# The columns of v as a seven-product unit behind q, gate and k in one pass of eight accumulators, the recurrence beside r

## The chip, the cores and the metric

One NeuronCore of one Trainium2 chip. The metric is the device time of one execution of the program, in microseconds.

## What is computed

A block with two branches of 1024 columns on 512 tokens of width 2048, everything in float32. The parts that matter here, cut from the reference:

```python
h = rms_norm(x, norm_g)                       # (512, 2048)
proj = h @ w_in                               # h, b, c, z of the convolution, then q, k (512 each), v, r (1024 each), gate (16)
# gated linear attention, 4 heads, chunks of 64 tokens
glog = log_sigmoid(g_down @ w_up + b_gate) / 16
bcum = cumsum(glog, within a chunk);  b_end = bcum[:, :, -1]
k_dec = k * exp(b_end - bcum)
u = einsum('bnchk,bnchv->bnhkv', k_dec, v)    # one state update for each chunk
state = exp(b_end) * state + u                # a scan over the 8 chunks
o = einsum('bnchk,bnhkv->bnchv', q, state)    # then RMS norm for each head, times silu(r)
# convolution branch: silu(z) * b * conv3(c * h);  both are joined, times w_out, plus x, then a final RMS norm
```

## The kernel before

Every projection is done to float32 accuracy with products of a reduced type: each operand is split into a high part (a rounding on ScalarE) and a low part (a subtraction on VectorE, lines 116 and 117), and three matmuls (high x high, low x high, high x low) take the place of one. The transposed, gain-scaled input h stands in SBUF all the time as `hT_hi` and `hT_lo`, 16 k tiles of 128 rows by 512 tokens. RMS norm's factor for a token, `rstd`, is applied to results.

The work goes in stages, one behind the other on TensorE:

1. *The time-major stage* (`w_tm`, line 262): gate, k and v, 16 + 512 + 1024 = 1552 columns. Tokens are the output's rows, so h is the stationary operand. The columns are cut into four passes of 388. A pass walks the 16 k tiles, with four accumulators (one bank for each 128 tokens), and the four passes alternate between the two groups of four banks. The first pass also loads x transposed (`load_x`), the second loads x by tokens for the sums of squares (`token_stats`), behind which `token_rstd` gives rstd and `tm_out` scales the results.
2. *q and r* (`ft_unit`, lines 157 to 159): 4 + 8 blocks of 128 columns, with the weights stationary and 512 tokens moving. After each half of a block `step()` runs one step of the generator `gla_steps`: six steps of gates and decays, then for each pair of chunks the state products (`pair_state`, u), the splits of the next k and v, and the outputs (`pair_out`, o), then their transposes (tp). It starts its first state products after seven half blocks, in the fourth block of q. r's blocks go to DRAM (`r_raw`).
3. *Four seven-product units* (`st_unit`, line 592), for z with b and c with h. A unit treats a 512 x 2048 by 2048 x 1024 product as 2 x 2 blocks and makes it with seven block products in place of eight: pa, pb and pc with blocks of the weights as loaded (`raw_mm`), then, in four steps c, the products pd, pe, pa and pf on weight blocks that VectorE mixes by sums and differences (line 646). Sums of blocks of h are needed for them (`quarter_sums`, four sets, made at the end of r from a second load of x): the operands s1, s2 and s4 are split and kept, and s3 is put in the place of the second token half of h's first eight k tiles (`place_third`), which nobody needs any longer. A unit's results leave by `gate_cols` or `conv_cols`. Before its last products a unit calls `before_out`, which splits the first weights of what comes next.
4. *The output projection* (`w_out`): 512 columns, a fifth seven-product unit for 1024, 512 columns again, and the final norm.

All DMAs of weights and of x are issued by SyncE's queue in order. Tiles of 128 x 512 come from one pool of 44 slots (`k2`), weights from 8 raw slots of 128 x 1024 and 4 slots each for their high and low parts (`SPLITBUFS`). PSUM's eight banks form two groups, `acc` and `aux`, of four. The text's order gives priorities; the framework's scheduler lays out each engine's queue from them when the program is built, and each engine serves its queue in that order. A tile that has no free slot waits for one.

Of the kernel before, what the change touches and what calls it, by code (L numbers as in the profile page):

```python
# [30 lines left out]
CH = 8  # L31
KPC = KT // CH
TMW = RANK + DK + GW
TMB = 4
TMC = TMW // TMB
UNIT = KPC * S
# [3 lines left out]
GST = 80  # L40
WARM = 9
# [3 lines left out]
STC = 4  # L45
HT = S // 2
# [3 lines left out]
def hybrid_block(ctx: ExitStack, tc: tile.TileContext, xT, x, params, w_tm, w_ft, w_st, w_up, b_gate, w_out, final_g, out):  # L50
# [68 lines left out]
    def raw_tile(name):  # L119
        return wpool.tile([P, UNIT], F32, tag="raw", name=f"raw_{name}", bufs=RAWBUFS)  # L120
# [16 lines left out]
    def load_split_fine(src, name):  # L137
        raw, (hi, lo) = raw_tile(name), split_tiles(name)

        def piece(i):  # L140
            sl = slice(i * TMC, (i + 1) * TMC)
            nc.sync.dma_start(out=raw[:, sl], in_=src[:, sl])
            (nc.scalar.copy if i else nc.vector.tensor_copy)(out=hi[:, sl], in_=raw[:, sl])
            nc.vector.tensor_sub(out=lo[:, sl], in0=raw[:, sl], in1=hi[:, sl].bitcast(F32))

        return hi, lo, piece

# [73 lines left out]
    def tm_out(b, pst):  # L221
        for tt in range(TT):
            c0 = b * TMC
            while c0 < (b + 1) * TMC:
                if c0 < RANK:
                    c1, dst = RANK, gd[:, tt, :]
                else:
                    j = (c0 - RANK) // S
                    c1 = min(RANK + (j + 1) * S, (b + 1) * TMC)
                    o0 = c0 - RANK - j * S  # L230
                    dst = kv[tt][j][:, o0 : o0 + c1 - c0]
                nc.vector.tensor_scalar(
                    out=dst, in0=pst[tt][:, c0 - b * TMC : c1 - b * TMC],
                    scalar1=rstd[:, tt : tt + 1], scalar2=None, op0=ALU.mult,
                )
                c0 = c1

    for b in range(TMB):
        pst = [(acc if b % 2 else aux)(f"tm{b}_{tt}") for tt in range(TT)]
        for c in range(CH):  # L240
            if b == 0:
                hi, lo, piece = load_split_fine(w_tm[b, c], f"tm{b}_{c}")
                for i in range(KPC):
                    if c == 0 and i == 0:
                        with tc.high_priority():
                            load_x(0)
                    else:
                        load_x(c * KPC + i)
                    piece(i)
            else:  # L250
                hi, lo = load_split(w_tm[b, c], KPC * TMC, f"tm{b}_{c}")
            if b == 1:
                for k in (2 * c, 2 * c + 1):
                    token_stats(*divmod(k, HC))
            for i in range(KPC):
                kt = c * KPC + i
                xh, xl = h(kt)
                csl = slice(i * TMC, (i + 1) * TMC)
                wh, wl = hi[:, csl], lo[:, csl]
                for k, (a, w) in enumerate(((xh, wh), (xl, wh), (xh, wl))):  # L260
                    for tt in range(TT):
                        nc.tensor.matmul(  # L262
                            pst[tt][:, 0:TMC], lhsT=a[:, tt * P : (tt + 1) * P], rhs=w,
                            start=kt == 0 and k == 0, stop=kt == KT - 1 and k == 2,
                        )
        if b == 0:
            first = pst
            gate_weights()
            continue
        if b == 1:  # L270
            token_rstd()
            tm_out(0, first)
            gate_inputs()
        tm_out(b, pst)


    rps = aux("rps")
# [6 lines left out]
    nc.tensor.matmul(rps, lhsT=onesr, rhs=dh, start=True, stop=False)  # L284
    nc.tensor.matmul(rps, lhsT=onesr, rhs=dl, start=False, stop=True)
    nc.scalar.copy(out=rB, in_=rps)


    def ft_unit(u):
# [146 lines left out]
    def gla_steps():  # L436
        ga = gate_transpose()
        yield
        gl = []
        for tt in range(TT):  # L440
            gl.append(gate(tt, ga))
            if tt % 2:
                yield
        for tt in range(TT):
            gate_decay(tt, gl[tt])
            if tt % 2:
                yield
        chunk_decays()
        chunk_splits(0)
        yield  # L450
        done = None
        for tt in range(TT):
            pair_state(tt)
            yield
            if done is not None:
                out_transpose(tt - 1, done)
            if tt + 1 < TT:
                chunk_splits(tt + 1)
            yield
            done = pair_out(tt)  # L460
            yield
        yield
        out_transpose(TT - 1, done)
# [27 lines left out]
    def r_block(b):  # L491
        r = ft_unit(HEADS + b)
        t1 = t2(f"r1_{b}")
        nc.vector.tensor_mul(out=t1, in0=r, in1=rB)
        nc.scalar.activation(t1, t1, AF.Silu)
        nc.sync.dma_start(out=r_raw[b], in_=t1)

    for hh in range(HEADS):
        q = ft_unit(hh)
# [9 lines left out]
        qs.append(parts)  # L509

# [24 lines left out]
    def quarter_sums(j):  # L535
# [7 lines left out]
        made = sums(*raws, j, "qs")  # L543
        for k in (4, 1, 2):
            s_parts[k][j] = split_small(made[k], f"qp{k}_{j}")
        s_parts[3][j] = made[3]

# [5 lines left out]

    for b in range(8):
        r_block(b)
        if b >= 6:
            for j in range(2):
                quarter_sums(2 * (b - 6) + j)
    for _ in steps:
        pass  # L560
# [13 lines left out]
    def st_source(u, c, q):  # L574
        return w_st[u, c, q] if u < 4 else w_out[1 + q % 2, STC * (q // 2) + c]
# [24 lines left out]
    def st_unit(u, factor, out, before_out, into=None, between=()):  # L600
        main, side = (aux, acc) if u % 2 else (acc, aux)
# [22 lines left out]
        if u == 0:  # L624
            for j in range(STC):
                place_third(j)
# [15 lines left out]
        for c in range(STC):  # L642
# [94 lines left out]
    def early_tail(f):  # L737
# [7 lines left out]
        return go  # L745

# [228 lines left out]
def _layout(x, norm_g, w_in, conv_w, conv_b, gla_w_up, gla_b_gate, gla_norm_g, w_out, final_g):  # L975
# [7 lines left out]
    tm = np.concatenate([g, k, v], axis=2)  # L983
    tm = tm.reshape(CH, KPC, P, TMB, TMC).transpose(3, 0, 2, 1, 4).reshape(TMB, CH, P, KPC * TMC)
# [9 lines left out]
    st = np.stack([unit(a[:, :, s], b[:, :, s]) for s in halves for a, b in ((cz, cbb), (cc, ch))])  # L994
# [42 lines left out]
```

## Time and profile before

| what | value |
|---|---|
| device time, median of 3 runs | 786.15 us (786.07 to 786.17) |
| the profiled execution: its own time, its span | 785.95 us, 783.6 us |
| TensorE busy, matmuls | 773.7 us, 3752 matmuls |
| VectorE, ScalarE, GpSimdE busy | 563.7, 379.9, 31.6 us |
| DMA | 140.39 MB, 179 GB/s over the span |

The span runs from the first to the last instruction; the profiled execution's own time is 2.35 us longer. Matmuls overlap in their pipeline, so a row's duration is longer than the distance to the next matmul. PE is TensorE, PEld its weight loads, DVE VectorE, ACT ScalarE, POOL GpSimdE, SP SyncE. A tile's name stands without its number.

### The profile page before, as it was taken

Reading aid. Unit: us, or ns where it says so; the run is one execution under the profiler, and the core shown is the slowest. Engines: PE = TensorE matmul, PEld = TensorE weight load, DVE = VectorE, ACT = ScalarE, POOL = GpSimd, SP = SyncE. Lnnn points to the kernel's source line nnn. Section 1 sums busy time; section 2 is a strip of 40 time slices with the busy share of each in tenths; the row PEclk is TensorE's granted clock in tenths of the full one; section 3 lists DMA queues with packets and bytes.
Section 4 is the critical chain, followed back from the end, with each engine's and each line's share of the span. In section 5 each row is a group of like instructions: output and inputs, shape, how many; then the busy total and the mean of one; then the engine's idle time right before and its main releaser. Section 6 shows DMA issues by size and latency. Waiting matters only on the chain.

```text
span 783.6 us, 10104 instructions
## 1 busy us (share of the span) xinstructions
PE 773.7 (99%) x3752; PEld 664.8 (85%) x3752; DVE 563.7 (72%) x711; ACT 379.9 (48%) x574; POOL 31.6 (4%) x38
## 2 busy tenths in 40 slices
PE   9999999999999999999999999999999999999995
PEld 9999999887878888888888888888888888888885
DVE  7533242366666549998998699878987997997913
ACT  6552121373688757644543445345436345733504
POOL 1000000000000000000000000000000000004601
PEclk9999999999999999999999999999999999999998
DMA  8973343222232238778866556665666459578006
GB/s 309 324 272 84 105 130 120 96 84 80 80 107 82 95 108 285 261 224 284 312 204 192 197 184 207 188 213 174 204 189 184 124 180 368 190 196 295 20 1 215
DMA packets 48932, 140.39 MB, mean 179 GB/s; under 512 B 5826, under 2 KB 7874, under 8 KB 48884
## 3 DMA queue, kind: packets, MB, share of 16 engines
q1 hardware_dynamic: 48628, 139.74, 54.3%
q8 instruction: 29, 0.48, 0.3%
q14 instruction: 19, 0.16, 0.1%
q10 hardware_dynamic: 256, 0.02, 0.0%
HBM read 130.29 MB, written 9.44 MB: 178 GB/s over the span
## 4 chain that ended last, share of the span: by engine, by line
PE 96%; ACT 1%; DVE 1%; issue 1%; POOL 0%; ACTq 0%; POOLq 0%
PE tm L262 17%; PE pa L592 14%; PE pc L592 7%; PE pb L592 7%; PE pf L592 7%; PE pe L592 7%; PE pd L592 7%; PE ft L159 5%; PE ft L157 5%; PE ft L158 5%; PE po L159 3%; PE po L158 3%; PE po L157 3%; PE u L363 1%; PE warm L86 1%
## 5 line engine op out<-in xcount | busy, mean ns | idle before, releaser
L116 ACT CAST hi_sq_t<-raw_sq 128x1024 fp32r<-128x1024 f32 x80 | 84.3, 1055 | 119.7 <-PE pf L592 24.0
L117 DVE TENSOR_TENSOR lo_sq_t<-raw_sq,hi_sq_t 128x1024 fp32r<-128x1024 f32 x80 | 98.4, 1234 | 20.5 <-ACT hi_sq_t L116 20.4
L646 DVE TENSOR_TENSOR raw_sq<-raw_sq,raw_sq 128x1024 f32<-128x1024 f32 x80 | 97.2, 1220 | 7.6 <-DMA raw_sq<-in_w_st 6.4
L116 ACT CAST hi_st<-raw_st 128x1024 fp32r<-128x1024 f32 x60 | 63.2, 1054 | 67.7 <-PE pa L592 21.6
L117 DVE TENSOR_TENSOR lo_st<-raw_st,hi_st 128x1024 fp32r<-128x1024 f32 x60 | 72.1, 1220 | 13.7 <-ACT hi_st L116 13.5
L157 PE MATMUL ft<-hhi,hi_ft 128*128 128x512 f32 x192 | 75.7, 394 | 0.0
L159 PE MATMUL ft<-hhi,lo_ft 128*128 128x512 f32 x192 | 75.2, 392 | 0.0
L158 PE MATMUL ft<-hlo,hi_ft 128*128 128x512 f32 x192 | 75.1, 391 | 0.0
L117 DVE TENSOR_TENSOR lo_tm<-raw_tm,hi_tm 128x776 fp32r<-128x776 f32 x24 | 23.2, 966 | 58.7 <-ACT hi_tm L116 58.7
L262 PE MATMUL tm<-hi_tm,hhi 128*128 128x388 f32 x256 | 56.3, 342 | 0.1
L262 PE MATMUL tm<-hi_tm,hlo 128*128 128x388 f32 x256 | 55.6, 339 | 0.0
L262 PE MATMUL tm<-lo_tm,hhi 128*128 128x388 f32 x256 | 55.4, 338 | 0.0
L116 ACT CAST hi_tm<-raw_tm 128x776 fp32r<-128x776 f32 x24 | 20.2, 842 | 68.2 <-PE tm L262 64.7
L117 DVE TENSOR_TENSOR lo_ft<-raw_ft,hi_ft 128x1024 fp32r<-128x1024 f32 x24 | 29.4, 1223 | 27.3 <-ACT hi_ft L116 27.2
L262 PEld LDWEIGHTS tm<-hi_tm,hhi 128*128 128x128 f32 x256 | 46.4, 190 | 0.7 <-ACT hhi L169 0.4
L262 PEld LDWEIGHTS tm<-lo_tm,hhi 128*128 128x128 f32 x256 | 46.0, 188 | 0.0
L262 PEld LDWEIGHTS tm<-hi_tm,hlo 128*128 128x128 f32 x256 | 45.9, 188 | 0.0
L159 PEld LDWEIGHTS ft<-hhi,lo_ft 128*128 128x128 f32 x192 | 36.0, 188 | 7.8
L157 PEld LDWEIGHTS ft<-hhi,hi_ft 128*128 128x128 f32 x192 | 36.1, 188 | 7.6 <-issue 0.2
L158 PEld LDWEIGHTS ft<-hlo,hi_ft 128*128 128x128 f32 x192 | 36.1, 188 | 7.3
L851 POOL TENSOR_TENSOR res<-res,fg 128x512 f32<-128x512 f32 x12 | 21.8, 1850 | 449.0 <-DMA fg<-in_final_g 443.0
L157 PE MATMUL po<-hi_wo,yh 128*128 128x512 f32 (+1 forms) x104 | 39.6, 381 | 0.0
(279 smaller groups left out, 1649.7 us busy)
## 6 DMA issues: line engine op xcount, KB each, us to landing
raw_sq<-in_w_st SPq DMA_DIRECT2D x64, 512.0 KB, 4.3
raw_st<-in_w_st SPq DMA_DIRECT2D x48, 512.0 KB, 4.4
raw_ft<-in_w_ft SPq DMA_DIRECT2D x24, 512.0 KB, 3.4
raw_tm<-in_w_tm SPq DMA_DIRECT2D x24, 388.0 KB, 4.1
raw_sq<-in_w_out SPq DMA_DIRECT2D x16, 512.0 KB, 4.1
raw_wo<-in_w_out SPq DMA_DIRECT2D x13, 512.0 KB, 3.9
raw_st<-in_w_out SPq DMA_DIRECT2D x12, 512.0 KB, 7.8
rawx<-in_xT SPq DMA_DIRECT2D x16, 256.0 KB, 4.8
```

What stands on the lines that cost most here:

```text
L86: nc.tensor.matmul(wps[:, 0:P], lhsT=ones, rhs=ones, start=True, stop=True)
L116: nc.scalar.copy(out=hi, in_=full)
L117: nc.vector.tensor_sub(out=lo, in0=full, in1=hi.bitcast(F32))
L157: nc.tensor.matmul(ps, lhsT=ah, rhs=bh, start=first, stop=False)
L158: nc.tensor.matmul(ps, lhsT=ah, rhs=bl, start=False, stop=False)
L159: nc.tensor.matmul(ps, lhsT=al, rhs=bh, start=False, stop=last)
L262: nc.tensor.matmul(pst[tt][:, 0:TMC], lhsT=a[:, tt * P : (tt + 1) * P], rhs=w, start=kt == 0 and k == 0, stop=kt == KT - 1 and k == 2,)
L363: nc.tensor.matmul(us[j][:, vsl], lhsT=kp[a][rows, ksl], rhs=vp[b][rows, vsl], start=k == 0, stop=k == 2)
L592: nc.tensor.matmul(ps[t], lhsT=fs[t][part_], rhs=ww[:, sl], start=first and c == 0 and r == 0 and k == 0, stop=last and c == STC - 1 and r ...
L646: nc.vector.tensor_tensor(out=dst, in0=x0, in1=x1, op=op)
L851: nc.gpsimd.tensor_mul(out=res[tt][cbk], in0=res[tt][cbk], in1=fg[cbk])
```

## The change

The time-major stage keeps gate and k only, 528 columns. It is one pass: two accumulators of 264 columns for each 128 tokens, so all eight banks, and each k tile is used for both. Weights come in groups of three pieces of 264 columns (the first two groups piece by piece). x by tokens is loaded from the sixth k tile on (`STATS0`). The last two k tiles are done bank by bank, and each bank is emptied behind its own last matmul, half of them by ScalarE.

The q heads follow, with one set of quarter sums behind each. Then v goes through `st_unit` with the number `UV` = 5; `v_cols` scales its results by rstd. Inside it `place_third` overwrites half of h's first eight k tiles, as in unit 0, and `restore_quarter` loads that quarter of x again and writes h back, one set after each step's product with s3. r's first block begins with the upper k tiles. The recurrence's generator has two empty steps more, so that its first state products fall behind the first half of r's first block, and the splits of the first k and v stand in front of r. The row of rstd (`rms_row`) moves into its first step. The quarter sums for units 0 to 3 are made again at the end of r, as before.

```diff
-TMW = RANK + DK + GW
-TMB = 4
+TMW = RANK + DK
+TMB = 2
 TMC = TMW // TMB
+TMP = KT * TMB
+TMG = 3
...
+UV = 5
...
-    kv = [[t2(f"kv{tt}_{j}") for j in range(3)] for tt in range(TT)]
+    kv = [[t2(f"k{tt}"), None, None] for tt in range(TT)]
     gd = const.tile([P, TT, RANK], F32, name="gd")
...
+    tm_group = [None, None]
...
+    def tm_weights(p):
+        g, i = divmod(p, TMG)
+        sl = slice(i * TMC, (i + 1) * TMC)
+        if i == 0:
+            raw, (hi, lo) = raw_tile(f"tm{g}"), split_tiles(f"tm{g}")
+            tm_group[:] = hi, lo
+            c0, n = p * TMC, min(TMG, TMP - p) * TMC
+            if g > 1:
+                nc.sync.dma_start(out=raw[:, 0:n], in_=w_tm[:, c0 : c0 + n])
+                split(hi[:, 0:n], lo[:, 0:n], raw[:, 0:n])
             else:
...
+                for j in range(TMG):
+                    fine = slice(j * TMC, (j + 1) * TMC)
+                    nc.sync.dma_start(out=raw[:, fine], in_=w_tm[:, c0 + j * TMC : c0 + (j + 1) * TMC])
+                    (nc.scalar.copy if j else nc.vector.tensor_copy)(out=hi[:, fine], in_=raw[:, fine])
+                    nc.vector.tensor_sub(out=lo[:, fine], in0=raw[:, fine], in1=hi[:, fine].bitcast(F32))
...
+        if b == 0:
+            nc.vector.tensor_scalar(out=dst, in0=src, scalar1=rstd[:, tt : tt + 1], scalar2=None, op0=ALU.mult)
+        else:
+            nc.scalar.activation(dst, src, AF.Copy, scale=rstd[:, tt : tt + 1])
...
+    tm_banks = [[(aux if b else acc)(f"tm{b}_{tt}") for tt in range(TT)] for b in range(TMB)]
+
+    def tm_mm(kt, b, tt, w):
+        xh, xl = h(kt)
+        for k, (a, wi) in enumerate(((xh, w[0]), (xl, w[0]), (xh, w[1]))):
+            nc.tensor.matmul(
+                tm_banks[b][tt][:, 0:TMC], lhsT=a[:, tt * P : (tt + 1) * P], rhs=wi,
+                start=kt == 0 and k == 0, stop=kt == KT - 1 and k == 2,
+            )
+
+    tm_last = {}
+    for kt in range(KT):
+        if kt == 0:
+            with tc.high_priority():
+                load_x(0)
+        else:
+            load_x(kt)
+        if kt == 2:
             gate_weights()
...
+        if STATS0 <= kt < STATS0 + 8:
+            for k in (2 * (kt - STATS0), 2 * (kt - STATS0) + 1):
+                token_stats(*divmod(k, HC))
+        for b in range(TMB):
+            w = tm_weights(kt * TMB + b)
+            if kt >= KT - 2:
+                tm_last[kt, b] = w
+            else:
+                for tt in range(TT):
+                    tm_mm(kt, b, tt, w)
...
+    token_rstd()
...
+    for b in range(TMB):
+        for tt in range(TT):
+            for kt in range(KT - 2, KT):
+                tm_mm(kt, b, tt, tm_last[kt, b])
+            tm_out(b, tt)
+        if b == 0:
+            gate_inputs()
+
+
+    def rms_row():
...
+    def ft_unit(u, first=0):
         ps = acc(f"ft{u}")
-        for half in range(2):
-            n = KT // 2
-            hi, lo = load_split(w_ft[u, half], UNIT, f"ft{u}_{half}")
+        n = KT // 2
+        for half in (int(first), int(not first)):
+            hi, lo = ft_weights(u, half)
             for i in range(n):
                 kt = half * n + i
                 csl = slice(i * P, (i + 1) * P)
-                mm3(ps, (hi[:, csl], lo[:, csl]), h(kt), kt == 0, kt == KT - 1)
+                mm3(ps, (hi[:, csl], lo[:, csl]), h(kt), half == first and i == 0, half != first and i == n - 1)
...
     def gla_steps():
+        rms_row()
...
         chunk_decays()
-        chunk_splits(0)
+        yield
+        yield
...
+        r = ft_unit(HEADS + b, b == 0)
...
-    for hh in range(HEADS):
-        q = ft_unit(hh)
+    def q_head(hh):
+        q = ft_unit(hh, 0)
...
+    def quarter_sums(j):
+        made = sums(*quarter_raws(j), j, "qs")
...
+    def restore_quarter(j):
+        raw = t2(f"rq{j}").rearrange("p (i t) -> p i t", i=2)
+        nc.sync.dma_start(out=raw, in_=xT[:, 2 * j : 2 * j + 2, HT:S])
+        for i in range(2):
+            kt = 2 * j + i
+            c, r = divmod(kt, HPC)
+            nc.scalar.activation(hT_hi[c][:, r, HT:S], raw[:, i, :], AF.Copy, scale=g_in[:, kt : kt + 1])
+            nc.vector.scalar_tensor_tensor(
+                out=hT_lo[c][:, r, HT:S], in0=raw[:, i, :], scalar=g_in[:, kt : kt + 1],
+                in1=hT_hi[c][:, r, HT:S].bitcast(F32), op0=ALU.mult, op1=ALU.subtract,
+            )
...
-        main, side = (aux, acc) if u % 2 else (acc, aux)
+        main, side = (aux, acc) if u in (1, 3) else (acc, aux)
...
-        if u == 0:
+        if u in (0, UV):
...
+            if u == UV:
+                restore_quarter(c)
...
+    def v_cols(i, j, ts):
+        for t in range(2):
+            tt = 2 * i + t
+            nc.vector.tensor_scalar(out=ts[t], in0=ts[t], scalar1=rstd[:, tt : tt + 1], scalar2=None, op0=ALU.mult)
+            kv[tt][1 + j] = ts[t]
+
+    def next_rows():
+        for half in (1, 0):
+            ft_weights(HEADS, half)
+
+    for hh in range(HEADS):
+        q_head(hh)
+        quarter_sums(hh)
+    ahead_of(UV)()
+    st_unit(UV, h_factor, v_cols, next_rows)
+    chunk_splits(0)
+    for b in range(8):
+        r_block(b)
+        if b >= 6:
+            for j in range(2):
+                quarter_sums(2 * (b - 6) + j)
+    for _ in steps:
+        pass
```

## Rows read from the trace of the kernel before

**Rows 1.** The page: the span, and busy time, share and instructions of each engine.

```profile
span 783.6 us, 10104 instructions
PE 773.7 (99%) x3752; PEld 664.8 (85%) x3752; DVE 563.7 (72%) x711; ACT 379.9 (48%) x574; POOL 31.6 (4%) x38
```

**Rows 2.** TensorE's waits: what it waited for, us in total, times, longest.

```profile
PE warm L86 <- POOL ones L83: 1.1, 1, 1.1
PE o L391 <- ACT oT L432: 0.7, 1, 0.7
```

**Rows 3.** The chain that ended last, in order of time: start us, us, what.

```profile
5.40 136.58 PE tm L262 x768
...
230.72 1.54 PE u L363 x12
...
250.09 1.62 PE u L363 x24
...
299.22 10.88 PE pa L592 x48
...
331.86 2.72 PE pd L592 x12
...
375.38 6.35 PE pa L592 x28
```

**Rows 4.** Timeline of TensorE: the time-major stage's ends, then a run of 256 columns.

```profile
5.40 1.39 PE L262 MATMUL tm<-hi_tm,hhi 128*128 128x388 f32 x4
...
9.67 0.86 PE L262 MATMUL tm<-lo_tm,hhi 128*128 128x388 f32 x4
...
141.81 0.40 PE L284 MATMUL rps<-dg_hi,onesr 128*128 128x512 f32 x1
...
735.33 0.28 PE L157 MATMUL po<-hi_wo,yh 128*128 128x256 f32 x1
...
736.76 0.40 PE L157 MATMUL po<-hi_wo,yh 128*128 128x512 f32 x1
```

**Rows 5.** By stretch: length; busy PE, PEld, DVE, ACT, POOL; clock, DMA share, GB/s.

```profile
5.40:40.00 34.60, 34.60 (x192) 34.33 (x193) 24.03 (x45) 21.54 (x40) 0.00 (x0) 1.00 0.96 343
735.33:736.76 1.43, 1.43 (x14) 1.43 (x13) 1.43 (x4) 1.43 (x5) 0.81 (x1) 1.00 0.00 0
142.45:299.22 156.77, 156.05 (x789) 128.25 (x789) 96.07 (x150) 102.58 (x206) 4.04 (x4) 1.00 0.29 92
299.22:375.38 76.16, 76.16 (x338) 63.06 (x337) 72.93 (x82) 41.45 (x51) 0.00 (x0) 1.00 0.83 275
```

**Rows 6.** Groups by line and form: ScalarE, then VectorE.

```profile
L541 ACT ACTIVATE raw_qx<-raw_qx,par 128x512 f32<-128x512 f32 x16 | 11.1, 728 | 3.3 <-DMA raw_qx<-in_xT 3.3
L184 ACT ACTIVATE rawt<-rawt 128x512 f32<-128x512 f32 x16 | 9.9, 621 | 0.0
L151 ACT CAST qp_hi<-qs 128x512 fp32r<-128x512 f32 x12 | 7.2, 616 | 3.1 <-DVE qs L526 3.1
...
L375 DVE SCALAR_TENSOR_TENSOR s<-s,decay,u 128x256 f32<-128x256 f32 x28 | 12.2, 474 | 0.0
...
L875 DVE TENSOR_SCALAR res<-res,rf 128x512 f32<-128x512 f32 x4 | 1.9, 487 | 2.6 <-POOL rf L868 2.6
```

**Rows 7.** Timeline of VectorE around the first seven-product unit.

```profile
288.38 0.69 DVE L494 TENSOR_TENSOR r<-ft,rB 128x512 f32<-128x512 f32 x1 [9.21 <-PE ft L159]
...
295.61 1.22 DVE L117 TENSOR_TENSOR lo_st<-raw_st,hi_st 128x1024 fp32r<-128x1024 f32 x1
...
321.80 0.68 DVE L152 TENSOR_TENSOR qp_lo<-qs,qp_hi 128x512 fp32r<-128x512 f32 x1
...
331.62 1.22 DVE L646 TENSOR_TENSOR raw_sq<-raw_sq,raw_sq 128x1024 f32<-128x1024 f32 x1
332.75 1.22 DVE L117 TENSOR_TENSOR lo_sq_t<-raw_sq,hi_sq_t 128x1024 fp32r<-128x1024 f32 x1
...
378.47 2.73 DVE L692 SCALAR_TENSOR_TENSOR c<-c,rstd,c 128x512 f32<-128x512 f32 x4
```

More of the change, by code (lines that the diff above doesn't have):

```diff
@@ L40 @@
 GST = 80
+STATS0 = 5
 WARM = 9
@@ L135, in load_split @@
         return split_weights(load_raw(src, n, name)[0], n, name)
[L137 to L146, printed above, removed]
     def split_small(t, name):
@@ L215, in gate_inputs @@
         nc.vector.tensor_sub(out=gst[:, :, 64:GST], in0=gd, in1=gh.bitcast(F32))
-    kv = [[t2(f"kv{tt}_{j}") for j in range(3)] for tt in range(TT)]
+    kv = [[t2(f"k{tt}"), None, None] for tt in range(TT)]
     gd = const.tile([P, TT, RANK], F32, name="gd")
[L221 to L249, printed above, removed]
-            else:
[L251 to L265, printed above, removed]
-        if b == 0:
-            first = pst
-            gate_weights()
[L269 to L274, printed above, removed]
@@ new lines, in tm_out @@
+    def tm_out(b, tt):
+        src = tm_banks[b][tt]
+        if b == 0:
+            nc.vector.tensor_scalar(
+                out=gd[:, tt, :], in0=src[:, 0:RANK], scalar1=rstd[:, tt : tt + 1], scalar2=None, op0=ALU.mult
+            )
+            dst, src = kv[tt][0][:, 0 : TMC - RANK], src[:, RANK:TMC]
+        else:
+            dst, src = kv[tt][0][:, TMC - RANK : DK], src[:, 0:TMC]
+        if b == 0:
+            nc.vector.tensor_scalar(out=dst, in0=src, scalar1=rstd[:, tt : tt + 1], scalar2=None, op0=ALU.mult)
+        else:
+            nc.scalar.activation(dst, src, AF.Copy, scale=rstd[:, tt : tt + 1])
@@ L283, in hybrid_block, with ft_weights @@
     dh, dl = split_small(dg, "dg")
[L284 to L289, printed above, removed]
+    for b in range(TMB):
[6 more added lines that the diff above has]
+    def rms_row():
+        rps = aux("rps")
+        nc.tensor.matmul(rps, lhsT=onesr, rhs=dh, start=True, stop=False)
+        nc.tensor.matmul(rps, lhsT=onesr, rhs=dl, start=False, stop=True)
+        nc.scalar.copy(out=rB, in_=rps)
+    ft_ahead = {}
+    def ft_weights(u, half):
+        if (u, half) not in ft_ahead:
+            ft_ahead[u, half] = load_split(w_ft[u, half], UNIT, f"ft{u}_{half}")
+        return ft_ahead[u, half]
+    def ft_unit(u, first=0):
         ps = acc(f"ft{u}")
-        for half in range(2):
-            n = KT // 2
-            hi, lo = load_split(w_ft[u, half], UNIT, f"ft{u}_{half}")
+        n = KT // 2
+        for half in (int(first), int(not first)):
+            hi, lo = ft_weights(u, half)
             for i in range(n):
@@ L533, in sums, with quarter_raws @@
         return made
-    def quarter_sums(j):
+    def quarter_raws(j):
         raws = []
@@ L542, in quarter_sums @@
             raws.append(raw)
-        made = sums(*raws, j, "qs")
+        return raws
+    def quarter_sums(j):
+        made = sums(*quarter_raws(j), j, "qs")
         for k in (4, 1, 2):
@@ L552, in place_third @@
         split(hT_hi[c][:, i : i + 2, HT:S], hT_lo[c][:, i : i + 2, HT:S], s)
[L554 to L560, printed above, removed]
     def h_factor(name, i, t):
@@ L574, in st_source @@
     def st_source(u, c, q):
-        return w_st[u, c, q] if u < 4 else w_out[1 + q % 2, STC * (q // 2) + c]
+        return w_st[min(u, 4), c, q] if u != 4 else w_out[1 + q % 2, STC * (q // 2) + c]
     def st_weights(u, c, q):
@@ L993, in _layout @@
     halves = [slice(0, S), slice(S, 2 * S)]
-    st = np.stack([unit(a[:, :, s], b[:, :, s]) for s in halves for a, b in ((cz, cbb), (cc, ch))])
+    st = [unit(a[:, :, s], b[:, :, s]) for s in halves for a, b in ((cz, cbb), (cc, ch))]
+    st = np.stack(st + [unit(*(v[:, :, s] for s in halves))])
     ft = np.concatenate([blocks(q), blocks(r)], axis=0)
```

8 lines of the change are left out of this document (4 added, 4 removed).

## The prediction

> **What bounds the kernel now.** I read the page's first lines first: TensorE is busy 773.7 of 783.6 us and no other engine is above 72% [rows 1]. A busy matmul engine need not be at its peak, so the next view is what it waited for: two entries, 1.8 us in all, one before the first matmul and one in the recurrence [rows 2]. So its queue is never starved, and the time is the sum, over matmuls, of the distance from one start to the next. The durations on the rows are no use for that sum, because they overlap (a 256-column matmul is drawn 0.28 long and the next begins 0.12 later [rows 4]); distances must be taken from starts, or from counts in the chain of waits.
>
> Three distances come out. In a seven-product unit, 12 matmuls of 512 columns take 2.72 us: 0.2267 each. From 299.22 to 375.38 one whole unit (336 of them) takes 76.16 us with nothing else in the chain [rows 3]. The time-major stage (gate, k and v, 388 columns each) takes 136.58 us for 768 matmuls [rows 3]; past its first 20, 748 matmuls run from 9.67 to 141.81, which is 0.1767 each, so the first 20, which take 4.27 instead of 3.53, lose 0.74 us [rows 4]. Near the end 12 matmuls of 256 columns, each with its own weight load, go from 735.33 to 736.76: 0.119 each [rows 4]. In the stretches looked at the granted clock is 1.00, the 2.4 GHz level [rows 5].
>
> **The change part by part.**
>
> *Time-major pass.* Its 768 matmuls become 2 x 16 x 3 x 4 = 384 of 264 columns. Price of one: between 256 columns (0.119) and 512 (0.2267) lies 0.42 ns a column, so 264 cost 0.1226. The same line gives 0.1746 at 388, where the stage shows 0.1767, so this stage may run 0.002 above it: 0.1247. I take the middle, 0.1236: 47.5 us, between 47.1 and 47.9.
>
> One reading speaks against the change. In the old stage the weight loads are busy 34.33 of 34.60 us [rows 5]; were they what paces it, at one per 0.1767 us, narrower matmuls would save nothing each and the pass would take 384 x 0.1767 = 67.9 us. The Trainium skill, in "Perfetto Trace Analysis", section "Identifying the Most-Contended Engine", says to judge how near TensorE is to its limit by the busy share of LDWEIGHTS and not of matmuls, which puts the old stage at its limit in loads. The stretch of 256 columns decides for the other reading: there the loads fill the window too (1.43 of 1.43 us [rows 5]), yet they come 0.119 apart. A load's drawn length stretches with the pace and does not set it. So 47.5 goes into the sum and 67.9 to a rival.
>
> *The start of that pass.* The first matmul still needs one x tile and one weight piece, now with three small weight loads ahead of the second x tile. The stretch from 5.4 to 40 us moved 343 GB/s [rows 5]. The new pass needs x, its transposed copy and 4.3 MB of weights, 12.7 MB in all, which is 37 us at that rate against 48 us of matmuls; the squares of x are loaded only from the sixth k tile on. Through the fifth tile it wants 2.7 MB, 8 us at that rate, while TensorE needs 15 us to use them. So nothing is late after the first tile. The loss at the start stays 0.7 by the old stage; were the second tile to miss its turn, it would be 3. I take 0.8, so the pass is 48.3 us.
>
> All eight banks stay taken until rstd is known. Rstd needs the squares of x: all loads up to the thirteenth tile, with the squares, are 11.1 MB, 32 us at that rate, and the squares are 16 operations of 0.62 on ScalarE [rows 6], while the last matmul is at 53 us. The last two k tiles are run bank by bank, so the other seven banks' matmuls cover the first evacuation. Cost: 0; without that cover q's first matmul would wait for two VectorE operations, about 1 us.
>
> *v as a seven-product unit.* 7 x 4 x 2 x 3 x 2 = 336 matmuls of 512 columns, as in unit 0: 76.16 us. That holds if VectorE and ScalarE keep up. VectorE's list: 28 weight splits and 16 mixes of 1024 elements, which start 1.13 apart when back to back [rows 7], 49.7; 14 adds, 4 placements of s3 and 7 operations of the last quarter sums at 0.60 apart (0.68 long less the same overlap [rows 6, 7]), 15.0; the restoring of h, 8 operations of 256 columns at 0.39 (0.47 less 0.08 [rows 6]), 3.1; scaling v by rstd, 8 at 0.41 (0.49 less 0.08, from the scaling of the output [rows 6]), 3.3. Together 71 of 76 us. SyncE's queue gets 28 weight loads of 524 KB and four of x, 262 KB each, for the restoring: 15.7 MB, or 206 GB/s, where unit 0 moved 275 [rows 5]. On VectorE unit 0 carried 72.93 of 76.16 [rows 5] with TensorE waiting for nothing [rows 2]. So no cost, with 5 us of room.
>
> The restoring itself costs TensorE nothing: tile c may be written once product s3 of step c is through, and the last one has two products (5.4 us) and the first half of r's block 0, which is turned round to begin with the upper rows (5.4 us), to be ready; it needs four operations of ScalarE and VectorE. The recurrence's first products come 5.4 us into r, when v's last quarter has just been scaled: the old adds and scalings of unit 0 end at 381.2, 5.8 us after its last product [rows 3, 7], so up to 1 or 2 us of waiting is possible here. I take 0.3.
>
> *Quarter sums a second time*, one set after each q head: 16 scalings (0.73) and 12 roundings (0.62) on ScalarE [rows 6], 28 operations of 0.68 on VectorE [rows 7], about 19 us on either beside q's 47 us of matmuls. Over the old q and r stretch VectorE was busy 96 and ScalarE 103 of 157 us [rows 5], so beside q alone it is nearly full and a set may spill into the unit, which the 71 us above count. Only the third operand group (s4) needs the sums, 21.8 us into the unit. In the old kernel the four sets ran on VectorE from 288 to 322 us, most of it inside unit 0, after the engine had stood 9.2 us [rows 7], and TensorE did not wait. Cost 0.
>
> *Recurrence beside r only.* Same matmuls; old q and r stretch 156.77 us [rows 5]. It starts and ends two half blocks later, inside r's block 6, where VectorE had stood 9.2 us [rows 7]. I leave the 156.77, with 3 us either way: the 96 state products (u) come 24 in 1.62 at one place and 12 in 1.54 at another [rows 3], as the order lets products of the two half arrays meet; all 96 cost 6.5 us at the one pace and 12.3 at the other, and the old order lies between.
>
> **Sum.** 136.58 goes; 48.3 + 76.16 + 0.3 = 124.8 comes: 11.8 us less. The profiled execution's own time is 785.95, its span 783.6 and 2.35 around it; it lies 0.2 below the median of the runs, 786.15. So 785.95 - 11.8 = 774.2.
>
> **The rivals.**
>
> *A, handovers.* TensorE waits at new seams: v's unit at its start, r's first products on v, the last quarter sums behind a later recurrence. Each seam is one in-order queue late by 1 to 4 us, so 776 to 784. For it: VectorE's 71 of 76 us leaves little; against it: unit 0 had the same load and no wait.
>
> *B, the other side: a queue behind q.* If all four sets of quarter sums stand ahead of the unit's first weight split on VectorE or ScalarE, TensorE has nothing for 20 us at the unit's start: 774 + 20 = 794. It decides from 12 us of pile-up on, that is from three of the four sets. It needs the engine's order to put them there, since queues are served in order. Against it: in the old order splits of unit 0's weights stood between operations of the sums (one at 295.61, before the unit began [rows 7]).
>
> *C, loads set the pace*, as worked out above: 20.4 us more, 794.6. The 256-column row speaks against it almost alone, but clearly.
>
> *D, the change doesn't deliver*: A's waits add up to the whole 11 to 13 us and the time stays within 0.2% of 786 (what a measurement can tell from no change here, 1.6 us).
>
> *E, better*: the state products all meet in pairs, and the stretch gives back 3 us: 771.
>
> **Chances.** The forecast (772 to 776) 0.63; A 0.21; E 0.05; B 0.05; C 0.03; D 0.03. So faster 0.89, same 0.03, slower 0.08. The range, 771.5 to 780, takes the bounds of the pass (47.1 to 47.9, start 0.7 to 3), the 3 us either way of the recurrence and the nearer half of A.
>
> **What would show it.** Right: the chain shows 384 tm matmuls in 47 to 49 us; the new unit as 28 products of 2.72 us with no piece of VectorE or ScalarE between; TensorE's waits still a few us; q and r together again about 157 us without the unit. Wrong: distances near 0.177 in the tm stage (C); VectorE or ScalarE in the chain within 10 us of the unit's start or end, with sums ahead of weight splits (B, A); a gap before the first product of the recurrence.

## The result, and the profile after

| | before | after |
|---|---|---|
| device time, median (lowest to highest) | 786.11 us (785.36 to 786.17), 4 runs | 776.18 us (773.96 to 777.93), 4 runs |
| the profiled execution: its own time, its span | 785.95, 783.6 us | 773.96, 772.1 us |

The ratio is 0.9874 with an interval of 0.9846 to 0.9903: the change is faster by 9.9 us at the medians, where 11.8 were forecast. The 774.2 forecast lies 2.0 below the median and next to the profiled run, which was the lowest of the four; the four spread over 4 us, where those of before spread over 0.8.

The page's first lines after, beside [rows 1]:

```profile
span 772.1 us, 10176 instructions
PE 759.9 (98%) x3704; PEld 638.5 (83%) x3704; DVE 619.4 (80%) x766; ACT 420.0 (54%) x635; POOL 32.0 (4%) x38
```

TensorE is still the one full engine, and VectorE has come up by 56 us. TensorE's waits, as [rows 2] (what it waited for: us in total, times, longest):

```profile
PE tm L252 <- ACT hhi L162: 1.8, 1, 1.8
PE warm L90 <- POOL ones L87: 1.1, 1, 1.1
PE o L408 <- ACT oT L449: 0.9, 1, 0.9
PE pa L620 <- DVE lo_st L121: 0.3, 1, 0.3
```

One entry is new and large: a wait in the time-major pass for `hhi`, the high part of an x tile. The chain that ended last, as [rows 3] (start us, us, what), shows where it comes from and that the new unit stands in the chain by its products alone:

```profile
5.99 5.45 DMA raw_tm<-in_w_tm
11.45 4.16 DMA rawx<-in_xT
15.63 0.73 ACT hhi L162
16.39 0.76 DVE hlo L163
17.19 37.54 PE tm L252 x308
...
102.19 7.25 PE pa L620 x32
109.78 3.87 PE pa L620 x16
113.65 10.88 PE pb L620 x48
...
135.41 2.72 PE pd L620 x12
...
176.21 2.72 PE pf L620 x12
```

From 17.19 on 308 matmuls of 264 columns take 37.54 us: 0.1219 each. The unit's products are 2.72 each from 135.41 to the last, with no piece of VectorE or ScalarE between. By stretch, as [rows 5] (length; busy PE, PEld, DVE, ACT, POOL; clock, DMA share, GB/s): the stretch in which TensorE stood idle (the hole), q, the unit, and r:

```profile
14.00:17.20 3.20, 1.35 (x10) 0.93 (x9) 2.82 (x5) 2.20 (x3) 0.00 (x0) 1.00 0.79 218
54.70:102.20 47.50, 47.50 (x212) 39.10 (x211) 30.19 (x42) 32.81 (x53) 0.00 (x0) 1.00 0.38 128
102.19:178.93 76.74, 76.74 (x341) 63.32 (x341) 72.48 (x88) 43.62 (x60) 0.00 (x0) 1.00 0.71 237
178.93:287.36 108.43, 107.45 (x577) 88.86 (x577) 77.46 (x126) 79.00 (x169) 4.04 (x4) 1.00 0.31 100
```

In the hole TensorE worked 1.35 of 3.20 us. What it waited for is seen in SyncE's queue after (start us, us, line, operation, tile):

```profile
5.04 0.43 SPq L161 DMA_DIRECT2D rawx<-in_xT  x1
5.51 0.91 SPq L223 DMA_DIRECT2D raw_tm<-in_w_tm  x2
6.53 0.36 SPq L191 DMA_DIRECT2D wup<-in_w_up  x1
...
9.11 1.47 SPq L223 DMA_DIRECT2D raw_tm<-in_w_tm  x2
11.45 1.28 SPq L161 DMA_DIRECT2D rawx<-in_xT  x3
```

The third x tile is sent at 5.04. The fourth is sent at 11.45, behind four weight groups and the gate's five small loads (`gate_weights`, which stands at the third k tile), lands at 15.61 by the chain, and is split by 17.2. TensorE had used up three k tiles by 14.6. By the chain the queue could send it only when a weight group sent at 5.99 had landed, at 11.43; from 5.04 to 11.45 the DMA engines were full (share 0.99, 325 GB/s).

**Where the time went**, by TensorE's starts in the two timelines. Up to the first `tm` matmul: 5.40 before, 4.92 after, -0.48. From there to q: 136.88 before, 49.65 after. The unit for v: 76.74 more. q and r: 156.78 before, 47.46 + 108.43 = 155.89 after, -0.89. From unit 0 to the end: 484.54 before, 484.90 after, +0.36. The sum is -11.5, the difference of the spans.

### The profile page after: what moved, and what is told of

Its sections match the earlier page's. It is cut to its first block, busy times and chain, and to the rows that moved or that the text cites. A ratio compares the mean times of both kernels' runs of the same rounds, so it can differ in the third digit from the quotient of the medians.

```text
span 772.1 us, 10176 instructions
## 1 busy us (share of the span) xinstructions
PE 759.9 (98%) x3704; PEld 638.5 (83%) x3704; DVE 619.4 (80%) x766; ACT 420.0 (54%) x635; POOL 32.0 (4%) x38
## 4 chain that ended last, share of the span: by engine, by line
PE 94%; ACT 1%; DMA 1%; DVE 1%; issue 1%; SPq 1%; POOL 0%; ACTq 0%; POOLq 0%; DVEq 0%
PE pa L620 17%; PE pc L620 8%; PE pf L620 8%; PE pe L620 8%; PE pd L620 8%; PE pb L620 8%; PE ft L151 5%; PE ft L150 5%; PE ft L152 5%; PE tm L252 5%; PE po L151 3%; PE po L150 3%; PE po L152 3%; PE u L380 1%; DMA raw_tm<-in_w_tm 1%
## 5 line engine op out<-in xcount | busy, mean ns | idle before, releaser
L121 DVE TENSOR_TENSOR lo_sq_t<-raw_sq,hi_sq_t 128x1024 fp32r<-128x1024 f32 x96 | 117.4, 1230 | 22.0 <-ACT hi_sq_t L120 21.8
L674 DVE TENSOR_TENSOR raw_sq<-raw_sq,raw_sq 128x1024 f32<-128x1024 f32 x96 | 116.4, 1219 | 6.0 <-DMA raw_sq<-in_w_st 5.2
L151 PE MATMUL po<-lo_wo,yh 128*128 128x512 f32 (+1 forms) x104 | 39.5, 379 | 0.0
L152 PE MATMUL po<-hi_wo,yl 128*128 128x512 f32 (+1 forms) x104 | 39.1, 379 | 0.0
L252 PE MATMUL tm<-hi_tm,hhi 128*128 128x264 f32 x128 | 36.1, 291 | 1.8 <-ACT hhi L162 1.8
L252 PE MATMUL tm<-lo_tm,hhi 128*128 128x264 f32 x128 | 35.8, 284 | 0.0
L252 PE MATMUL tm<-hi_tm,hlo 128*128 128x264 f32 x128 | 35.7, 283 | 0.0
L120 ACT CAST hi_ft<-raw_ft 128x1024 fp32r<-128x1024 f32 x24 | 25.2, 1049 | 15.0 <-PE ft L151 9.7
L252 PEld LDWEIGHTS tm<-hi_tm,hhi 128*128 128x128 f32 x128 | 24.1, 193 | 2.2 <-ACT hhi L162 2.0
L620 PE MATMUL pa<-lo_st,hhi 128*128 128x512 f32 x80 | 24.9, 392 | 0.3 <-DVE lo_st L121 0.3
```

Source lines behind the costliest of these rows:

```text
L120: nc.scalar.copy(out=hi, in_=full)
L121: nc.vector.tensor_sub(out=lo, in0=full, in1=hi.bitcast(F32))
L151: nc.tensor.matmul(ps, lhsT=ah, rhs=bl, start=False, stop=False)
L152: nc.tensor.matmul(ps, lhsT=al, rhs=bh, start=False, stop=last)
L252: nc.tensor.matmul(tm_banks[b][tt][:, 0:TMC], lhsT=a[:, tt * P : (tt + 1) * P], rhs=wi, start=kt == 0 and k == 0, stop=kt == KT - 1 and k ...
L620: nc.tensor.matmul(ps[t], lhsT=fs[t][part_], rhs=ww[:, sl], start=first and c == 0 and r == 0 and k == 0, stop=last and c == STC - 1 and r ...
```

## Experiments

All times are medians, with the lowest and highest run; ratios are to the kernel before, run on the same chip. The part of each edit that matters is shown.

**The change again.** No edit.

> The changed kernel once more, for the spread of its times (773.96 to 777.93 in four runs, where the kernel before spread over 0.8 us) and for a second profile. Theory: the spread comes from the first 20 us, where the profile of after has TensorE waiting 1.8 us for one x tile that was sent late behind other loads; then this profile has a hole of another length at the same place and nothing else differs by more than 0.3 us. Rival: the clock dips in some executions at other places; then the hole is 1.8 us again and a stretch later on is longer at a granted clock below 1.00.

777.98 us (774.57 to 779.44), ratio 0.9891 (0.9872 to 0.991). Its profiled run has the hole in the same place and of the same length: from the last matmul at full pace to the next one 3.1 us, 15.15 to 18.27 here and 14.31 to 17.42 in the first profile. What differs is a wait of 1.1 us for a piece of weights ten us earlier, and the clock behind the hole. TensorE's waits, and then single matmuls of its timeline (start us, us) as the clock falls and comes back:

```profile
PE tm L252 <- ACT hhi L162: 1.6, 1, 1.6
PE tm L252 <- ACT hi_tm L229: 1.1, 1, 1.1
```

```profile
16.99 0.74 PE L252 MATMUL tm<-hi_tm,hhi 128*128 128x264 f32 x4 [1.55 <-ACT hhi L162]
...
18.27 0.28 PE L252 MATMUL tm<-lo_tm,hhi 128*128 128x264 f32 x1
18.39 0.28 PE L252 MATMUL tm<-hi_tm,hlo 128*128 128x264 f32 x1
...
19.97 0.42 PE L252 MATMUL tm<-hi_tm,hhi 128*128 128x264 f32 x1
20.19 0.42 PE L252 MATMUL tm<-hi_tm,hlo 128*128 128x264 f32 x1
...
22.35 0.28 PE L252 MATMUL tm<-lo_tm,hhi 128*128 128x264 f32 x1
22.47 0.28 PE L252 MATMUL tm<-hi_tm,hhi 128*128 128x264 f32 x1
```

```profile
19.00:20.00 1.00, 1.00 (x7) 1.00 (x6) 0.87 (x2) 0.68 (x1) 0.00 (x0) 0.50 0.95 336
23.00:24.00 1.00, 1.00 (x10) 1.00 (x10) 0.14 (x1) 1.00 (x4) 0.00 (x0) 1.00 1.00 377
```

The same matmul comes 0.12 after its forerunner at 18.4, 0.22 at 20.2, and 0.12 again at 22.5; the windows (columns as above) show the granted clock at 0.50, the 1.2 GHz level, and back at 1.00. From 18.88 to 22.17 there are 15 distances of 0.22: 1.5 us lost, on top of the holes. In the first profiled run, with one wait of 1.8, the clock stayed at 1.00. The pass took 51.91 us here and 49.65 there: 0.7 of the difference is the earlier wait (the sixth matmul starts 2.12 us behind the first here and 1.43 there), 1.5 the clock. So the rival came nearer than the theory: the hole did not change, the clock did, though right behind the hole and not at another place.

**The gate's loads late.** `gate_weights()` at the third k tile from the end.

```diff
-        if kt == 2:
+        if kt == KT - 3:
             gate_weights()
```

> The loads of the decay gate's weights, five small ones, move from the third k tile to the fourteenth; nothing else changes. Theory: standing among the first loads they held back the fourth x tile (sent at 11.45 us, behind four weight groups), and TensorE ran dry from 14.4 to 17; then the fourth x tile is sent before 8 us, the hole goes, the time-major pass takes 47.5 to 48.3 us in place of 49.5, the time is about 1.8 us less than that of the changed kernel, and its runs lie within 1 us of each other. Rival: DMA bandwidth at the start sets it (325 GB/s at a share of 1.0); then the wait only moves to another tile and the time stays within 0.5 us of the changed kernel.

773.59 us (772.65 to 773.92), ratio 0.9835 (0.9823 to 0.9848). The fourth x tile now leaves right behind the third, at 5.5. The pass takes 47.51 us, its wait is down to 0.2, and the runs lie within 1.3 us of each other. That is 4.4 below the run of the change beside it, more than twice the 1.8 expected: that figure counted the wait of one profile and not the clock.

**x ahead.** The gate's loads stay, but three x tiles pass them.

```diff
-        else:
+        elif kt < 3 or kt > 5:
             load_x(kt)
         if kt == 2:
+            for ahead_kt in (3, 4, 5):
+                load_x(ahead_kt)
             gate_weights()
```

> The gate's five small loads stay behind the third x tile, but the fourth, fifth and sixth x tiles are sent ahead of them; the weight groups three and four then come behind the small loads. It parts two readings of the hole in the first 20 us. Theory: the x tile's place in SyncE's queue was the fault; then the hole goes as with the gate's loads moved away, the time-major pass takes 47.5 to 48.5 us and the runs lie within 1.5 us of each other near 773.5. Rival: the five small loads themselves are the fault, each holding one of the few places for loads under way; then TensorE now runs dry for the third weight group, about as long, and the time is again 774 to 779.

773.04 us (772.12 to 773.87), ratio 0.9831 (0.9814 to 0.9847). SyncE's queue now sends four x tiles at 5.02, ahead of the small loads, and the stretch of the hole is full (29 matmuls, 3.20 of 3.20 us):

```profile
5.02 1.85 SPq L161 DMA_DIRECT2D rawx<-in_xT  x4
7.12 0.34 SPq L191 DMA_DIRECT2D wup<-in_w_up  x1
```

```profile
14.00:17.20 3.20, 3.20 (x29) 3.20 (x28) 1.97 (x2) 0.98 (x2) 0.00 (x0) 1.00 0.77 197
```

The small loads are still there and TensorE no longer waits in that stretch, so it was the x tile's place in the queue, not the small loads as such. Nor was it the rate: from 5.04 to 11.45 the DMA engines are as full here (share 0.97, 303 GB/s) as in the change.

In the profiled executions little of this is left at the end: spans of 771.7 and 772.3 in the two runs with x ahead, 772.1 in the change, whose profiled execution was its fastest and kept its clock. The pass is 1.9 and 1.5 us shorter, but TensorE waits longer among the first products of unit 1, where it waited 0.3 in the change:

```profile
PE pa L622 <- DVE lo_st L121: 1.2, 1, 1.2
```

It is 1.5 in the second profile, 1.0 with the gate late, and none in the second profile of the change, so whether the earlier start causes it is not shown.

**Both cures**, and the last one again as a measure beside it.

> The three x tiles ahead (as in the run with x ahead) and the gate's small weights moved to the third k tile from the end (as in the run with the gate late), together. Theory: both cure the same hole, that of the fourth x tile near 15 us, so together they give no more than the better one: 772.5 to 773.5, and a spread under 2 us. Rival: the small loads cost something by themselves also when x is ahead; then the pair is 1 us or more below the run with x ahead, 772 or less.

> The kernel with x ahead once more, as the measure for the two others of this call: 772 to 774. Nothing is changed against its first run.

773.93 us (772.96 to 774.34), ratio 0.9846 (0.9833 to 0.986), for both; 773.18 (772.52 to 774.12), ratio 0.9839 (0.9826 to 0.9853), for x ahead alone. The pair lies 0.4 above what was expected and not below x ahead alone. The two cures do not add: they cure one hole.

**Eight products.** v behind q in two plain passes of 512 columns, 384 matmuls, without quarter sums and without restoring h.

> v is made behind q by a plain product: two passes of 512 columns over all k tiles, 384 matmuls of 512 columns, in place of the seven-product unit's 336; no quarter sums beside q, no placing and restoring of h. All else as in the changed kernel. Theory: the gain is the eighth block product that is left out; then v takes 384 x 0.2267 = 87.1 us in place of 76.2, and the time is about 785, no more than 1.5 us below the kernel before. Rival: the gain comes from the wider matmuls and the other order (fewer matmuls, fewer weight loads, recurrence beside r); then the time stays near 774 to 778 and VectorE is far less busy.

787.3 us (785.37 to 789.87), ratio 1.0017 (1.0004 to 1.003). v takes 87.04 us by the chain, against 76.74 as a unit:

```profile
105.70 87.04 PE pv L797 x384
```

87.04 / 384 = 0.2267, and the eighth block product is 48 such matmuls, 10.9 us, of which 10.3 show. The wider tiles alone are worth little: 46.8 for the pass and 87.04 for v make 133.8 beside the old stage's 136.58, and the start takes that back: the pass took 52.55 here, with a wait of 3.1 and behind it the lower clock once more:

```profile
18.50:21.50 3.00, 3.00 (x16) 3.00 (x14) 1.68 (x3) 2.72 (x7) 0.00 (x0) 0.50 0.87 291
```

That is why the time came out 2.3 above the 785 expected.

**Half the width.** Each matmul of the pass as two of 132 columns, 768 instead of 384.

```diff
-            nc.tensor.matmul(
-                tm_banks[b][tt][:, 0:TMC], lhsT=a[:, tt * P : (tt + 1) * P], rhs=wi,
+            for n0 in (0, TMC // 2):
+                n1 = n0 + TMC // 2
+                nc.tensor.matmul(
+                    tm_banks[b][tt][:, n0:n1], lhsT=a[:, tt * P : (tt + 1) * P], rhs=wi[:, n0:n1],
```

> Each matmul of the time-major pass, 264 columns, is issued as two of 132 with a weight load each: 768 in place of 384, the same products. It prices the weight load, on which the rival of the 0.1767 us pace rested. Theory: the distance is set by columns as long as a load is hidden, and by the load where it isn't, at the 0.109 us of the transposes of 128 columns (8 in 0.87 us); then the pass takes about 768 x 0.109 = 84 us in place of 48, and the time is some 35 us more, about 810. Rival 1: columns alone (0.067 us each): 52 us, about 778. Rival 2: loads at 0.1767: 136 us, about 862.

811.67 us (811.66 to 811.96), ratio 1.0322 (1.0309 to 1.0336). The pass takes 86.37 us, 0.1125 for each of the 768. In its middle, 60 us hold 540 matmuls, 0.111 each, and the weight loads fill the window:

```profile
20.00:80.00 60.00, 60.00 (x540) 60.00 (x539) 17.94 (x27) 29.09 (x58) 1.03 (x1) 1.00 0.58 208
```

Half the columns bring the distance from 0.122 to 0.111 and no lower. Here, and only here, something else than columns sets the pace, at 0.11 for a matmul and its load. It is no floor for every matmul: four small ones of the recurrence (dp), whose loads have 8 rows, start 0.06 to 0.09 apart behind 109.37 in the profile after. That it is the load of 128 rows fits what was expected; no run parts it from another cost of such a pair. The four runs lie within 0.3 us: a slower TensorE finds its x tile there.

**v first.** The unit directly behind the pass, q behind it: q no longer covers the quarter sums.

```diff
     for hh in range(HEADS):
-        q_head(hh)
         quarter_sums(hh)
     ahead_of(UV)()
-    st_unit(UV, h_factor, v_cols, next_rows)
+    st_unit(UV, h_factor, v_cols, next_q)
+    for hh in range(HEADS):
+        q_head(hh)
```

> v's unit stands directly behind the time-major pass, in front of q, with its quarter sums beside that pass; q's first block then begins with the upper k tiles in place of r's. It takes q's 47 us of cover away from the quarter sums and tests rival B (a queue of sums ahead of the unit's weights). Theory: only s4, 21.8 us into the unit, needs the sums, so the cover is worth little: the unit takes at most 2 us more and the time stays within 2 us of the changed kernel. Rival B: sums, reloads of x and weight splits pile up at the seam and TensorE waits 10 us or more, 785 and above.

783.15 us (781.78 to 786.01), ratio 0.9964 (0.9947 to 0.998): 5.2 us above the second timing of the change, between what the two expected. The largest wait is at the unit's start, and ScalarE's queue shows why (start us, us, line, operation):

```profile
PE pa L620 <- ACT hi_st L120: 4.6, 1, 4.6
```

```profile
55.45 0.90 ACT L245 ACTIVATE k<-tm,rstd 128x264 f32<-128x264 f32 x2
...
58.86 0.72 ACT L561 ACTIVATE raw_qx<-raw_qx,par 128x512 f32<-128x512 f32 x1
59.48 0.61 ACT L144 CAST qp_hi<-qs 128x512 fp32r<-128x512 f32 x1
60.04 1.04 ACT L120 CAST hi_st<-raw_st 128x1024 fp32r<-128x1024 f32 x1
```

The unit's first weight cast stands behind the emptying of the pass's banks and behind scalings and roundings of the sums. So the queue of the prediction's rival B exists as soon as q is gone, at a quarter of its price. The clock fell behind this hole too (0.83 on average from 60 to 70 us), and the unit took 78.64.

**Ballast in v's unit.** Extra VectorE operations of 512 columns on a tile that nobody uses, 0.60 each, between the mixes: four for each step c.

```diff
             mix(b22, ALU.subtract, b22, b11)
+            for i in range(4 if u == UV else 0):
+                half = b11[:, (i % 2) * S : (i % 2 + 1) * S]
+                nc.vector.tensor_tensor(out=ballast, in0=half, in1=ballast, op=ALU.max)
             w1 = parts(b11, 1)
```

> In the seven-product unit of v, VectorE gets 16 operations of 512 columns more, four in each of the last four steps, at 0.60 us apart 9.6 us in all; their results go nowhere. It tests the step that VectorE's 71 of 76 us leave 5 us of room. Theory: the sum decides; 71 + 9.6 is 4 to 5 us over, so the unit takes about 81 us in place of 76.7 and the time grows by some 4 us against the changed kernel. Rival 1: what counts is each step of 10.88 us with 9.9 us of VectorE's own work, and the lead from before is used up at once; then 1.4 us a step, 5.7 us in all. Rival 2: the unit has far more room than the list says and nothing changes.

786.5 us (783.96 to 788.63), ratio 1.0 (0.9988 to 1.0012). Against the first profile of the change the unit is 6.3 longer and r 3.2: 9.5 of 9.6 lost, more than any of the three readings expected. Taken alone this said that VectorE has no room at all; smaller weights, on the kernel with x ahead, were needed to see where the loss begins.

> The kernel with x ahead, and in v's unit one extra VectorE operation of 512 columns for each of the four steps (4 x 0.60 = 2.4 us, and one copy ahead of the unit, 0.4), where the heavier ballast had four for each step. Theory: VectorE's room is counted step by step (about 9.9 of 10.88 us taken), so 0.6 more for each step still fits: 0 to 0.5 us against the kernel with x ahead in this call, and no new wait of TensorE in the unit. Rival: there is no room at all, each added us is lost as 9.5 of 9.6 were: 2.4 to 2.8 us slower, with waits on mixed weights in the unit or at r's start.

> The kernel with x ahead, and in v's unit two extra VectorE operations of 512 columns for each of the four steps (8 x 0.60 = 4.8 us, and one copy ahead of the unit, 0.4). Theory of room step by step (about 9.9 of 10.88 us taken, so 1.0 for each step): 1.2 added for each step is 0.2 over, so 0.5 to 1.5 us against the kernel with x ahead (773.1), the first waits of TensorE on mixed weights. Rival, five us of room in the whole unit: nothing lost, 773.

> The kernel with x ahead, and in v's unit four extra VectorE operations of 512 columns for each of the four steps (16 x 0.60 = 9.6 us): the heavy ballast again, now without the hole at the start. Theory of room step by step: 2.4 for each step is 1.4 over, 4 x 1.4 = 5.6 lost, and up to 3 more from what comes late behind the unit: 778 to 782. Rival, each added us is lost once the engine is full: 9.5 lost, 782 to 783.

| added to VectorE | device time | against x ahead (773.18) | the unit | VectorE busy in it |
|---|---|---|---|---|
| 0 | 773.18 us (772.52 to 774.12) | | 76.79 us | 71.70 us |
| 2.8 | 772.94 (771.68 to 773.53) | -0.2 | 76.73 | 74.51 |
| 5.2 | 774.79 (772.49 to 775.08) | +1.6 | 78.49 | 75.62 |
| 10.0 | 781.92 (781.9 to 782.92) | +8.7 | 83.12 | 79.62 |

The first 2.8 us cost nothing: they go into VectorE's idle time. Of 10.0, the unit's idle time took 1.6 (from 5.1 down to 3.5), 2.1 were pushed behind the unit, and 6.3 made it longer; the part pushed behind it met the recurrence, and r took 111.5 where it had taken 108.6. With 10.0 added, TensorE's waits are on the casts of mixed weights and on the recurrence:

```profile
PE pf L622 <- ACT hi_sq_t L120: 1.6, 2, 1.2
PE tp L448 <- ACT o L439: 1.4, 2, 0.7
PE pa L622 <- ACT hi_sq_t L120: 1.1, 2, 0.6
```

Where VectorE scales v's last rows in its timeline, first with 10.0 added, then without:

```profile
189.96 2.46 DVE L785 TENSOR_SCALAR c<-c,rstd 128x512 f32<-128x512 f32 x6
```

```profile
181.55 2.46 DVE L782 TENSOR_SCALAR c<-c,rstd 128x512 f32<-128x512 f32 x6
```

r begins at 183.58 and at 177.40, so v comes 6.4 us behind r's start and not 4.2.

The rival with no room at all falls by the row of 2.8. At 5.2 the loss is just above what counting step by step expected, and against the rival with 5 us for the whole unit it speaks only weakly: the ratio is 0.985 (0.9837 to 0.9864), and the intervals overlap. The profiles speak more clearly: the unit is 1.7 longer, and TensorE's first wait on a mixed weight is there (0.6, for `hi_sq_t`), which the run with 2.8 does not have. At 10.0 step and rival expected nearly the same, and 781.92 does not choose between them.

## Why the prediction was right, and which terms were mis-sized

*The time-major pass by starts.* Right: 0.1219 for 264 columns, where 0.1236 was taken and 0.1226 to 0.1247 given as ends. So the line through [rows 4] holds by itself; the 0.002 that the old stage ran above it did not come along. 384 of them are 46.8, 0.7 less than the 47.5.

*Weight loads.* Rival C is out, but not for the reason given: "A load's drawn length stretches with the pace" is wrong. After the change loads fill the window at 0.122 (below, 22.00 of 22.00 us), as they did at 0.1767 in [rows 5], and in the run with half the width they fill it at 0.111.

```profile
30.00:52.00 22.00, 22.00 (x184) 22.00 (x183) 14.68 (x29) 15.93 (x29) 1.03 (x1) 1.00 1.03 397
```

Single loads, though, are drawn equally long at all three paces (ns, least/median/most; before, after, half the width):

```profile
L262 PEld LDWEIGHTS tm<-hi_tm,hlo x208: 187/188/189, 19.9 to 130.0; 128*128 128x128 f32 x104
L252 PEld LDWEIGHTS tm<-lo_tm,hhi x70: 187/188/189, 24.9 to 49.9; 128*128 128x128 f32 x70
L254 PEld LDWEIGHTS tm<-lo_tm,hhi x180: 192/192/192, 20.0 to 79.8; 128*128 128x128 f32 x180
```

So loads that come less than 0.188 us apart overlap as drawn and fill the window, whatever sets the pace; at the 0.2267 of a unit they fill 0.83 of it, 63.06 of 76.16 us [rows 5]. The conclusion of the prediction holds, its reason does not. The Trainium skill's measure ("Perfetto Trace Analysis", section "Identifying the Most-Contended Engine"), the busy share of LDWEIGHTS, one of two that it names for TensorE, was at its full value in all three. Only distances at two widths told them apart: from 388 to 264 columns the distance falls with the columns, from 264 to 132 it hardly does.

*The start of the pass: the step that failed.* "So nothing is late after the first tile" was reckoned from bytes: 2.7 MB through the fifth tile, 8 us at 343 GB/s. The rate was about as reckoned (325); the order was not. Four weight groups, two of them for the seventh k tile and later, and five loads that each took the queue a few hundred nanoseconds went ahead of the fourth x tile while the DMA engines were full (share 0.99): it was sent at 11.45, not at the 5.5 at which both cures send it. The loss is 49.65 - 46.8 = 2.8 us in the first profiled run and 5.1 in the second (1.5 of it the clock), where 0.8 was taken; the prediction had a bound of 3 for such a turn missed, but at the second tile. With x ahead the loss is 1.4 or less (47.75 and 48.15 in its two profiled runs), and the medians are 773.0 and 773.2. So the medians of 776.2 and 778.0 come from this term, together with the lower clock that follows it in some executions; how they share it is known only for the profiled ones.

*The end of the pass.* Right as far as rows show: q's first matmul starts at 54.57, 0.12 behind the last of the pass.

*v's unit.* 76.74, where 76.16 and 0.3 of handover were said; no wait of TensorE inside it, and no handover either: the 0.6 above 76.16 lies at four small matmuls of the recurrence (dp) that fell into it (0.34, and 0.2 in the two distances beside them). VectorE was counted at 71 us and measured 72.48 and 71.70. "5 us of room" was right as idle time and too large as room: about 3 can be had for nothing, while 5.2 made the unit 1.7 longer in the profiled run.

*Quarter sums at no cost.* Right, and the cover named for them was the right one: without q ahead of the unit they and the emptying of the banks cost about 5 us.

*q and r as before.* -0.9, or -1.0 like for like, since two matmuls for the row of rstd (0.46) have moved there and the four of dp (0.34) out of it. It leans to case E: 68 state products in the chain added up to 6.35 us before and 5.70 after. Taken over all starts of both stretches, the 96 state products took 7.83 us before and 7.19 after, so this is 0.6 of the 1.0; q's and r's own matmuls took 134.34 and 133.83, the outputs o 7.74 and 8.11. The prediction put the 96 between 6.5 and 12.3; at 7.83 no more than 1.3 was to be had, so E's 3 us was mis-sized.

*Rivals.* A's band begins at 776, and the median of 776.18 lies just inside it and 0.2 above the forecast's own. But its cause is not A's: what A said of TensorE waiting at v's start and at r's first products did not come (0.3 among the first products of unit 1, 0.9 in the recurrence, where [rows 2] had 0.7); the late tile is a handover of A's kind at a seam that A did not name. B and D did not come. That seven products are what pays, and not the width of the tiles, was shown by the plain eight: 10.3 us of v's time, and 9.3 between the medians of that run and of the change beside it.

*The sum.* That the profiled execution, 773.96, met the 774.2 is in part luck. Against the terms of the sum the pass is 1.05 longer and the unit 0.28; q and r are 0.89 shorter, the time to the first matmul 0.48 shorter, and the rest 0.36 longer. These misses add up to 0.3.

## What to carry to other kernels

Where a stage gets faster at its very start, look at the order in the queue that feeds it, not only at the bytes: a load of a few hundred nanoseconds put where it reads well can hold back a tile that TensorE needs. Time a dense matmul stream by distances between starts at two widths; the busy share of matmuls and of weight loads were both full here at 0.177, at 0.122 and at 0.111, since each load is drawn 0.19 long. And room on a second engine can be less than its idle time (here about 3 of 5 us): add a known weight in two or three sizes and see where the time begins to rise.

## Not expected of the hardware

Five profiled executions have the hole near 15 us. In three of them (the change again, eight products, ballast) the granted clock fell to 0.50, the 1.2 GHz level, for some 3.4 us close behind it, at a cost of 1.5 us in the change again; in two (the first profile, v first) it stayed at 1.00 there. The wait for the x tile alone does not decide it: 1.6, 3.1 and 3.0 us where the clock fell, 1.8 and 3.1 where it did not. The three had also waited 0.6 to 1.1 us for weights some 10 us before, the two at most 0.3; that this decides is not shown.

Kernels with the hole spread widely from run to run, the change over 4.0 and 4.9 us; the four sets of runs without hole and ballast over 1.3 to 1.8. The mean granted clock of the runs goes with this: with eight products the four slowest (788.9 to 789.9 us) had 0.992 and the three fastest (785.4 to 786.2) 0.996 to 0.998, while all runs of those four sets had 0.996 to 0.998. Estimated from these figures, 0.005 of 786 us is 3.9 us of clock, so 8 us at half of it, which at 0.22 in place of 0.122 us a matmul costs some 3.5 us; the two groups lie 3.7 apart. In the change itself the order is not so strict (779.05 at 0.996), so the clock is not all of its spread.

Halving the columns of a matmul from 264 to 132, each with its own weight load, took the distance only from 0.122 to 0.111 us.
